# A decoder layer on one core: wide operands for part of the gate/up products, and a new order

## The chip, the cores and the metric

The kernel runs on one core of a Trainium2 chip. A core has engines with instruction streams of their own: TensorE (PE in the profile; its weight loads are PEld), VectorE (DVE), ScalarE (ACT), GpSimd (POOL) and SyncE (SP), which issues most DMAs. The metric is the device time of one execution in microseconds. Lower is better.

## The reference

One layer, float32, on 512 tokens of width 1024: a half-step SwiGLU FFN, two attention groups of eight heads each (native sparse attention and stick-breaking attention) with one output projection, cross-attention to a memory of 256 tokens, and a second half-step FFN.

```python
def swiglu(h, wg, wu, wd):
    return (jax.nn.silu(h @ wg) * (h @ wu)) @ wd
...
x = x + 0.5 * swiglu(rms_norm(x, ffn1_norm[l]), ffn1_wg[l], ffn1_wu[l], ffn1_wd[l])
h = rms_norm(x, mix_norm[l])
...
x = x + jnp.concatenate([o_nsa, o_sb], axis=-1) @ w_out[l]
x = x + memory_cross_attention(rms_norm(x, mem_x_norm[l]), ...)
x = x + 0.5 * swiglu(rms_norm(x, ffn2_norm[l]), ffn2_wg[l], ffn2_wu[l], ffn2_wd[l])
```

The FFNs' inner width is 2816, which is 22 blocks of 128 columns.

## The kernel before

**Precision.** Activations and weights are kept transposed, with 128 channels on the partitions. A float32 operand is split into a high part, rounded to TensorE's fp32r type by a copy on ACT, and a low part, the rest, by a subtraction on DVE (`wsplit`, L580, for weights). One product is three matmuls (`mm3`, L629): high x high, high x low (both with the weight's high part as stationary operand) and low x high.

**Direct blocks.** `ffn_up` (L825) computes a block of gate and up with eight 128-row steps each, three matmuls of 512 columns per step.

**Winograd blocks.** Most blocks of gate and up go through `wino_up` (L904), a seven-product scheme of the Strassen-Winograd kind: the 1024 inner rows are cut in two halves, the 512 tokens in two halves, and gate and up are the two output rows. `right` (L842) makes the seven activation operands b11, b21, b22, t1 to t4 from the normed input, for four steps d each, in two halves ("a" needs the first 256 tokens, "b" all). The weight sums s1 to s4 are DVE additions. `prod` (L886) runs four steps of `mm3` with 256 columns each. The products go to three PSUM banks: X takes b11, then t2, then t3 on top of each other; Y takes b21 and t4 in its two halves; Z takes t1 and then b22. Between them the kernel reads X and Z into SBUF (`take`, L944, and the additions after it), by ACT copies or DVE additions of 256 columns. For 16 blocks of the second FFN the gate's two products (b11, b21) are made early by `wino_gate` (L891).

**Down products.** `ffn_down` (L964) multiplies a group of finished blocks (GROUPS, L68) with one of eight weight units and adds to x.

**Order.** Nothing runs in the order written. A `Planner` (L122 to L521) collects all operations, simulates engines with costs in ns, and emits one fixed instruction order per engine; this is why nearly all instructions carry line 521. Priorities come from the order in which parts are listed: FIRST (L28) for the direct blocks and the operands a0 to b3 of the first FFN, FEED (L71) for the blocks, down products ("0.4" is group 0, unit 4) and stored units ("cw:7") of each FFN, MIDDLE (L83) for attention and the early gates of the second FFN. In FEED a block with a number below that of the direct blocks is skipped. A stored unit (`store_parts`, L592) is loaded and split during the first FFN, and its parts are written to DRAM; later `unit` (L603) loads the parts without splitting.

**PSUM.** Eight banks: two of kind "mm" (X, odd down products), five of "at" (Y, Z, even down products and the attention), one of "sm".

Of the kernel before, what the change touches and what calls it, by code (L numbers as in the profile page):

```python
# [9 lines left out]
F32R = mybir.dt.float32r  # L10
# [17 lines left out]
FIRST = "up up a0 a1 up up b1 up a3 a2 b2 b0 b3"  # L28
# [39 lines left out]
GROUPS = {"1": (6, 8, 8), "2": (8, 8, 6)}  # L68


FEED = {"1": """6 5 ws:1 0.4 cw:7 0.3 18 9 7 wn:1 13 0.5 11 20 10 cw:6 12 0.1 mo:0 0.7 0.2 cw:2 14 0.6 0.0 cw:4 8 17  # L71
15 cw:1 19 1.4 mo:1 1.7 mq:0 16 ws:0 21 1.5 1.1 1.2 ws:2 2.2 1.0 cw:0 mn 2.0 1.3 wn:0 2.7 1.6 2.5 mq:1 2.4 2.1 ws:3 mk
cw:3 2.3 wn:2 2.6 mv wn:3 cw:5""",
        "2": """3 10 4 5 1 2 7 0 6 20 19 0.2 15 0.5 11 17 8 0.4 0.6 16 9 0.1 14 12 13 0.0 1.6 1.0 0.3 1.1 21 1.2 18 2.2 1.5
0.7 2.0 1.3 1.4 2.6 1.7 2.5 2.3 2.1 2.4 2.7"""}
# [7 lines left out]
MIDDLE = """sb_proj.2 sb_values sb_head.2.0 sb_head.2.1 rope sb_proj.3 cmp_mlp.0 sb_proj.0 sb_head.3.1 sb_head.3.0  # L83
sb_head.0.1 cmp_keys sb_proj.1 sb_head.1.1 nsa_query.1 nsa_query.2 nsa_query.3 sb_head.1.0 nsa_query.0 sb_head.0.0
query_rotate nsa_key.1 nsa_key.0 key_rotate cmp_mlp.1 nsa_values nsa_scores.0.0 nsa_scores.1.0 cmp_values
nsa_scores.1.1 nsa_compressed.1 nsa_compressed.2 nsa_scores.0.1 nsa_out.1.1 nsa_compressed.0 nsa_scores.2.0
nsa_out.0.1 nsa_out.0.0 nsa_scores.3.1 nsa_out.1.0 nsa_scores.2.1 nsa_out.2.1 wout_sb wout_nsa.0 nsa_out.2.0
nsa_compressed.3 nsa_scores.3.0 nsa_out.3.1 mem_query.0.0 nsa_out.3.0 mem_query.0.1 mem_head.0.0.1 mem_head.0.1.1
mem_head.0.0.0 mem_head.0.1.0 mem_out.0 wout_nsa.1 right.0.0 right.0.1 mem_query.1.1 right.0.2 right.0.3 gate.15
mem_head.1.1.1 mem_query.1.0 mem_head.1.0.0 mem_head.1.0.1 mem_head.1.1.0 gate.18 gate.8 gate.1 gate.10 mem_out.1  # L90
gate.16 gate.17 gate.6 gate.19 gate.20 gate.11 gate.21 gate.14 right.1.0 gate.13 right.1.1 gate.9 gate.12 right.1.2
right.1.3"""
# [38 lines left out]
class Planner:  # L131
# [15 lines left out]
    NEAR = 20  # L147
    DMA_NS, DMA_GBPS, STORE = 2700, 300, 1.6
# [189 lines left out]
    def attempt(self, hold):  # L338
# [33 lines left out]
        port = {}  # L372

# [27 lines left out]
        while len(out) < len(ops):  # L401
            for e in engines:
                while busy[e] <= now:
# [39 lines left out]
                    if e == "tensor":  # L443
                        tick = int(now / self.TICK_NS)
                        if columns.get(tick - 1, 0) < self.TICK_COLUMNS:
                            ns *= 2
                        columns[tick] = columns.get(tick, 0) + op.columns
# [76 lines left out]
class Kernel:  # L524
# [317 lines left out]
    def right(self, B, gcol, r, half, d):  # L842
# [17 lines left out]
        for i, e in enumerate((d, d + 4)):  # L860
            nc.vector.scalar_tensor_tensor(h[:, i * H:(i + 1) * H], self.x[e][:, hc], self.gm[:, gcol + e:gcol + e + 1],
                                           r[:, hc], OP.mult, OP.mult)
        if half == 0:
            B["h", d] = h
            q = self.pair()
            parts(h, *q)
            B["b11", d], B["b21", d] = [t[:, :H] for t in q], [t[:, H:] for t in q]
            return
        b11, b21, b12, b22 = B["h", d][:, :H], B["h", d][:, H:], h[:, :H], h[:, H:]
        if ("b22", d ^ 1) not in B:  # L870
            B["b22", "both", d // 2] = self.pair()
        B["b22", d] = [t[:, d % 2 * H:(d % 2 + 1) * H] for t in B["b22", "both", d // 2]]
        parts(b22, *B["b22", d])
# [6 lines left out]
        for src, n0, n1 in ((t12, "t1", "t2"), (t34, "t3", "t4")):  # L880
            q = self.pair()
            parts(src, *q)
            B[n0, d] = q[0][:, :H], q[1][:, :H]
            B[n1, d] = q[0][:, H:], q[1][:, H:]

    def prod(self, ps, w, B, b, first=True):  # L886
        for i in range(4):
# [90 lines left out]
    def ffn(self, k, B, As, early, pre, done):  # L978


        for part in FEED[k].split():
# [11 lines left out]
            elif n >= pre:  # L993
                self.wino_up(k, n, B, As[n], early.get(n))
# [891 lines left out]
```

## Time and profile before

| | |
|---|---|
| median of three runs | 1064.45 us (1062.35 to 1064.98) |
| profiled execution: its span from the first to the last instruction (the page gives no other time of it) | 1060.7 us |
| mean granted TensorE clock | 0.994 |
| PE busy | 1042.9 us, 6708 matmuls |
| weight loads busy | 948.3 us, 6708 |
| DVE busy | 906.6 us, 1904 instructions |
| ACT busy | 660.8 us, 1383 instructions |
| HBM | 136.40 MB read, 23.07 MB written |

The first FFN fills the span to about 340 us, the middle goes to about 700, early gates and the second FFN fill the rest. Matmuls are pipelined, so the recorded length of one is longer than its distance from the next; distances between starts say what one costs. Records of DVE and ACT instructions in a row overlap a little as well. A row of a timeline is: start in us, length in us, engine, line, operation, output<-inputs by the program's names (p is PSUM, t an SBUF tile, w and raw weight tiles, half a half-width tile), partitions x elements, and the count of instructions merged into it.

### The profile page before, as it was taken

The page shows a single profiled execution, that of the slowest core. Times are in us where ns is not written, and L with a number is a line of the kernel's source. Part 1 is how long each engine was busy: PE and PEld are TensorE (multiplying, and loading weights), DVE is VectorE, ACT ScalarE, POOL GpSimd, SP SyncE. Part 2 cuts the span into 40 slices and gives each one's busy share as a digit, 9 for nine tenths or more (in the row PEclk, how much of TensorE's full clock was granted, in tenths as well). Part 3 has the DMA queues.
Part 4 walks back from the last instruction along what each step waited for, and adds up shares of the span by engine and source line. Part 5 has one row for each costly group of instructions (what it writes and reads, how often), then busy time and mean ns, then how long its engine had stood idle before and what let it go on. Part 6 is the DMA issues. An engine that isn't in the chain of part 4 may idle for free.

```text
span 1060.7 us, 19227 instructions
## 1 busy us (share of the span) xinstructions
PE 1042.9 (98%) x6708; PEld 948.3 (89%) x6708; DVE 906.6 (85%) x1904; ACT 660.8 (62%) x1383; POOL 47.3 (4%) x88
## 2 busy tenths in 40 slices
PE   9999999999999999899989999999999999999998
PEld 7899999998988888788878889899999999998887
DVE  8998988898956977988899988899999999885632
ACT  8565665565744858889867868787566545452420
POOL 0000000000000000000003442110000000000000
PEclk9999999999999999999989999999999999999999
DMA  8336537548767833510357263356333444442321
GB/s 278 104 97 203 174 114 249 179 150 281 247 229 244 290 98 118 192 59 10 120 159 230 61 218 121 111 175 210 110 123 120 130 149 134 132 143 86 119 93 50
DMA packets 92881, 162.06 MB, mean 153 GB/s; under 512 B 11248, under 2 KB 17008, under 8 KB 92784
## 3 DMA queue, kind: packets, MB, share of 16 engines
q1 hardware_dynamic: 92352, 160.54, 47.2%
q8 instruction: 53, 0.87, 0.3%
q14 instruction: 44, 0.36, 0.1%
q10 hardware_dynamic: 432, 0.29, 0.1%
HBM read 136.40 MB, written 23.07 MB: 150 GB/s over the span
## 4 chain that ended last, share of the span: by engine, by line
PE 85%; DVE 8%; DMA 3%; ACT 2%; issue 1%; SPq 0%; ACTq 0%; DVEq 0%
PE p L521 85%; DVE t L521 4%; DVE s L521 2%; ACT t L521 2%; DMA raw<-in_ws_dram 2%; DMA d<-w 1%; DVE w L521 1%; DVE raw L521 1%; ACT w L521 0%; DVE gates L521 0%; SPq L521 0%; ACTq L521 0%; ACT L516 0%; DVEq L521 0%
## 5 line engine op out<-in xcount | busy, mean ns | idle before, releaser
L521 PE MATMUL p<-t,w 128*128 128x256 f32 (+1 forms) x5502 | 885.0, 319 | 4.5 <-ACT t L521 1.7
L521 PEld LDWEIGHTS p<-t,w 128*128 128x128 f32 x5502 | 780.5, 190 | 75.9 <-DVE t L521 4.3
L521 ACT ACTIVATE w<-raw 128x512 fp32r<-128x512 f32 (+1 forms) x450 | 267.7, 613 | 204.2 <-PE p L521 123.1
L521 DVE TENSOR_TENSOR w<-raw,w 128x512 fp32r<-128x512 f32 (+1 forms) x450 | 295.5, 671 | 78.6 <-issue 27.8
L521 ACT ACTIVATE t<-t 128x512 f32<-128x512 f32 (+7 forms) x424 | 214.2, 533 | 68.0 <-DVE t L521 63.8
L521 DVE TENSOR_TENSOR t<-t,t 128x512 fp32r<-128x512 f32 (+8 forms) x332 | 186.8, 578 | 10.6 <-ACT t L521 8.7
L521 ACT ACTIVATE t<-p 128x256 f32<-128x256 f32 (+5 forms) x156 | 75.2, 504 | 37.4 <-PE p L521 35.7
L521 PE MATMUL p<-t,t 128*128 128x256 f32 (+4 forms) x450 | 93.7, 333 | 0.4 <-ACT t L521 0.3
L521 DVE SCALAR_TENSOR_TENSOR t<-p,t 128x512 f32<-128x512 f32 (+3 forms) x107 | 66.3, 629 | 29.0 <-PE p L521 24.5
L521 DVE TENSOR_TENSOR t<-p,t 128x256 f32<-128x256 f32 (+4 forms) x159 | 82.2, 536 | 7.9 <-PE p L521 3.7
L521 PEld LDWEIGHTS p<-t,t 128*128 128x128 f32 x450 | 71.4, 190 | 10.0 <-ACT t L521 1.6
L521 DVE TENSOR_TENSOR raw<-raw,raw 128x512 f32<-128x512 f32 (+1 forms) x94 | 59.1, 635 | 0.9
L521 DVE TENSOR_TENSOR t<-p,half 128x256 f32<-128x256 f32 x117 | 45.8, 416 | 4.9 <-PE p L521 2.3
L521 POOL TENSOR_SCALAR t<-t,s 128x256 f32<-128x256 f32 (+3 forms) x80 | 44.6, 580 | 110.8 <-DVE s L521 48.9
L521 PE MATMUL p<-w,t 128*128 128x512 f32 (+2 forms) x240 | 40.8, 330 | 0.2 <-DVE s L521 0.2
L521 PEld LDWEIGHTS p<-w,t 128*128 128x128 f32 x240 | 36.3, 189 | 4.1 <-issue 0.4
L521 PE MATMUL p<-cr,t 128*128 128x128 f32 (+2 forms) x256 | 37.9, 265 | 0.2 <-ACT t L521 0.2
L521 ACT ACTIVATE w<-w 128x512 fp32r<-128x512 f32 x39 | 24.5, 627 | 20.3 <-DVE w L521 11.8
L521 PEld LDWEIGHTS p<-cr,t 128*128 128x128 f32 x256 | 31.3, 152 | 3.6 <-ACT t L521 0.6
L521 ACT ACTIVATE t<-t,g 128x256 fp32r<-128x256 f32 (+1 forms) x40 | 23.5, 587 | 13.7 <-DVE t L521 11.7
L521 PE MATMUL p<-t,cr 128*128 128x512 f32 (+4 forms) x114 | 30.5, 332 | 0.5 <-DVE t L521 0.5
L521 ACT ACTIVATE half<-p 128x256 f32<-128x256 f32 x46 | 17.3, 377 | 17.6 <-PE p L521 17.3
(82 smaller groups left out, 439.8 us busy)
## 6 DMA issues: line engine op xcount, KB each, us to landing
raw<-in_ws_dram SPq DMA_DIRECT2D x364, 256.0 KB, 3.0
w<-d SPq DMA_DIRECT2D x112, 256.0 KB, 3.2
d<-w SPq DMA_DIRECT2D x80, 256.0 KB, 3.9
raw<-in_wraw_dram SPq DMA_DIRECT2D x16, 256.0 KB, 3.0
raw<-in_ws_dram SPq DMA_DIRECT2D x22, 128.0 KB, 3.0
t<-in_xT_dram SPq DMA_DIRECT2D x8, 256.0 KB, 4.9
out_dram<-t SPq DMA_DIRECT2D x7, 256.0 KB, 2.0
t<-in_memT_dram SPq DMA_DIRECT2D x8, 128.0 KB, 4.4
```

The source lines that it names most:

```text
L521: return getattr(getattr(self.nc, op.eng), method)(*args, **kw)
```

## The change

A new table WIDE names, per FFN and block, which banks become wide: "x" is X, "z" is X and Z, "-" none. The activation operands now lie in one 512-column tile each, high part on the left, low part on the right. For a wide bank a step of `prod` issues one matmul of 512 columns (the weight's high part against both parts) and one of 256 (the weight's low part against the high part, added to the right half). The left half of the bank then holds the sums and the right half the corrections, and `whole` adds the two while it evacuates. `right` splits its results in halves of 256 columns, each into a tile of its own. FIRST has six "up" instead of five, so 16 blocks of the first FFN instead of 17 go through Winograd; 15 of them and 8 of the second FFN are wide somewhere, 23 in all. GROUPS of the second FFN is cut 8, 7, 7 instead of 8, 8, 6. FEED, MIDDLE and the list of stored units (qn:3 is new among them) have a new order; FEED's block 0 to 5 entries of the first FFN are skipped. The planner's cost of a 256-column matmul after a wide one is 6 ns less. The assertions check only the order of the lists.

```diff
--- before.py
+++ after.py
@@ -25,7 +25,7 @@
 NCMP = 31
 
 
-FIRST = "up up a0 a1 up up b1 up a3 a2 b2 b0 b3"
+FIRST = "up a0 up up up a1 b1 a3 up a2 up b2 b3 b0"
 NBIG = 74
 NWARM = 7
 KEEP = 4
@@ -65,14 +65,17 @@
            "compressed": "vector", "softmax": "gpsimd", "abs": "vector scalar",
            "double": "vector scalar gpsimd"}
 
-GROUPS = {"1": (6, 8, 8), "2": (8, 8, 6)}
-
-
-FEED = {"1": """6 5 ws:1 0.4 cw:7 0.3 18 9 7 wn:1 13 0.5 11 20 10 cw:6 12 0.1 mo:0 0.7 0.2 cw:2 14 0.6 0.0 cw:4 8 17
-15 cw:1 19 1.4 mo:1 1.7 mq:0 16 ws:0 21 1.5 1.1 1.2 ws:2 2.2 1.0 cw:0 mn 2.0 1.3 wn:0 2.7 1.6 2.5 mq:1 2.4 2.1 ws:3 mk
-cw:3 2.3 wn:2 2.6 mv wn:3 cw:5""",
-        "2": """3 10 4 5 1 2 7 0 6 20 19 0.2 15 0.5 11 17 8 0.4 0.6 16 9 0.1 14 12 13 0.0 1.6 1.0 0.3 1.1 21 1.2 18 2.2 1.5
-0.7 2.0 1.3 1.4 2.6 1.7 2.5 2.3 2.1 2.4 2.7"""}
+GROUPS = {"1": (6, 8, 8), "2": (8, 7, 7)}
+
+
+WIDE = {"1": "zzx--xxxxxxxxx-xxxxxxz", "2": "-x--x-x----xz---zzx---"}
+
+
+FEED = {"1": """0 wn:1 3 ws:0 10 14 mo:1 8 18 0.4 cw:7 0.3 7 13 6 ws:1 0.5 20 9 cw:6 12 4 11 0.7 2 mo:0 cw:2 0.6 0.2 0.1 0.0 cw:4 19
+17 cw:1 15 1.4 wn:0 1.5 16 1.2 1 mq:0 21 5 1.7 2.2 1.1 1.0 mn cw:0 1.3 2.0 ws:2 mk qn:3 2.7 2.5 2.4 mq:1 2.1 1.6 2.3
+cw:3 wn:2 ws:3 2.6 mv wn:3 cw:5""",
+        "2": """3 4 10 7 0 5 2 1 6 21 0.2 14 11 0.5 12 0.6 16 15 0.7 9 8 0.1 0.3 20 17 13 1.2 19 1.6 0.0 1.5 18 1.4 2.2 0.4 1.0 1.3
+2.4 2.0 1.1 2.3 2.5 1.7 2.1 2.7 2.6"""}
 
 UNITS = [("1g", NF), ("1u", NF), ("1d", ND * len(GROUPS["1"])), ("vs", 4), ("sq", 4), ("sk", 4), ("ks", 1), ("kw", 1), ("vg", 4),
          ("kc", 1), ("vc", 1), ("qn", 4), ("ws", 4), ("mk", 2), ("mv", 2), ("wn", 4), ("mq", 2), ("mo", 2),
@@ -80,16 +83,15 @@
 UNIT_AT = {n: sum(k for _, k in UNITS[:i]) for i, (n, _) in enumerate(UNITS)}
 
 
-MIDDLE = """sb_proj.2 sb_values sb_head.2.0 sb_head.2.1 rope sb_proj.3 cmp_mlp.0 sb_proj.0 sb_head.3.1 sb_head.3.0
-sb_head.0.1 cmp_keys sb_proj.1 sb_head.1.1 nsa_query.1 nsa_query.2 nsa_query.3 sb_head.1.0 nsa_query.0 sb_head.0.0
-query_rotate nsa_key.1 nsa_key.0 key_rotate cmp_mlp.1 nsa_values nsa_scores.0.0 nsa_scores.1.0 cmp_values
-nsa_scores.1.1 nsa_compressed.1 nsa_compressed.2 nsa_scores.0.1 nsa_out.1.1 nsa_compressed.0 nsa_scores.2.0
-nsa_out.0.1 nsa_out.0.0 nsa_scores.3.1 nsa_out.1.0 nsa_scores.2.1 nsa_out.2.1 wout_sb wout_nsa.0 nsa_out.2.0
-nsa_compressed.3 nsa_scores.3.0 nsa_out.3.1 mem_query.0.0 nsa_out.3.0 mem_query.0.1 mem_head.0.0.1 mem_head.0.1.1
-mem_head.0.0.0 mem_head.0.1.0 mem_out.0 wout_nsa.1 right.0.0 right.0.1 mem_query.1.1 right.0.2 right.0.3 gate.15
-mem_head.1.1.1 mem_query.1.0 mem_head.1.0.0 mem_head.1.0.1 mem_head.1.1.0 gate.18 gate.8 gate.1 gate.10 mem_out.1
-gate.16 gate.17 gate.6 gate.19 gate.20 gate.11 gate.21 gate.14 right.1.0 gate.13 right.1.1 gate.9 gate.12 right.1.2
-right.1.3"""
+MIDDLE = """sb_proj.2 sb_values sb_head.2.0 sb_head.2.1 sb_proj.3 rope cmp_mlp.0 sb_proj.0 sb_head.3.1 sb_head.3.0 sb_head.0.1
+cmp_keys sb_proj.1 sb_head.1.1 nsa_query.2 nsa_query.1 nsa_query.3 sb_head.1.0 nsa_query.0 sb_head.0.0 query_rotate
+nsa_key.1 nsa_key.0 cmp_mlp.1 key_rotate nsa_values nsa_scores.0.0 nsa_scores.1.1 nsa_scores.1.0 cmp_values
+nsa_compressed.1 nsa_out.1.1 nsa_scores.0.1 nsa_compressed.2 nsa_compressed.0 nsa_scores.2.0 nsa_out.0.0 nsa_out.0.1
+nsa_out.1.0 nsa_scores.3.1 nsa_scores.2.1 wout_sb nsa_out.2.1 wout_nsa.0 nsa_out.2.0 nsa_compressed.3 nsa_scores.3.0
+nsa_out.3.1 nsa_out.3.0 mem_query.0.1 mem_query.0.0 mem_head.0.0.1 mem_head.0.1.0 mem_head.0.1.1 mem_head.0.0.0
+mem_out.0 wout_nsa.1 right.0.0 right.0.1 right.0.3 mem_query.1.1 right.0.2 gate.15 mem_query.1.0 mem_head.1.0.0
+mem_head.1.0.1 mem_head.1.1.0 gate.18 mem_head.1.1.1 gate.1 mem_out.1 gate.16 gate.6 gate.8 gate.19 gate.11 gate.17
+gate.14 right.1.0 gate.13 gate.20 right.1.1 gate.9 gate.21 right.1.3 gate.12 gate.0 right.1.2"""
 
 
 HOLD = """sb_head.3.0>sb_head.3.1 sb_head.1.1>sb_head.3.0"""
@@ -145,6 +147,7 @@
 
     ROWS_NS = {"vector": 115, "scalar": 118, "gpsimd": 112}
     NEAR = 20
+    HIDDEN_NS = 6
     DMA_NS, DMA_GBPS, STORE = 2700, 300, 1.6
 
     TICK_NS, TICK_COLUMNS = 10240 / 3, 3060
@@ -370,6 +373,7 @@
         columns = {}
         rows = {e: (0, 0) for e in engines}
         port = {}
+        wide = False
 
         def fits(op):
             new = [n for n in op.tiles if n not in opened]
@@ -441,6 +445,9 @@
                             ns += self.ROWS_NS[e]
                         rows[e] = op.rows
                     if e == "tensor":
+                        if wide and op.columns == T // 2:
+                            ns -= self.HIDDEN_NS
+                        wide = op.columns >= T
                         tick = int(now / self.TICK_NS)
                         if columns.get(tick - 1, 0) < self.TICK_COLUMNS:
                             ns *= 2
@@ -860,43 +867,69 @@
         for i, e in enumerate((d, d + 4)):
             nc.vector.scalar_tensor_tensor(h[:, i * H:(i + 1) * H], self.x[e][:, hc], self.gm[:, gcol + e:gcol + e + 1],
                                            r[:, hc], OP.mult, OP.mult)
+        def both(src, n0, n1):
+            for n, t in ((n0, src[:, :H]), (n1, src[:, H:])):
+                q = self.t2(F32R)
+                parts(t, q[:, :H], q[:, H:])
+                B[n, d] = q
+
         if half == 0:
             B["h", d] = h
-            q = self.pair()
-            parts(h, *q)
-            B["b11", d], B["b21", d] = [t[:, :H] for t in q], [t[:, H:] for t in q]
+            both(h, "b11", "b21")
             return
         b11, b21, b12, b22 = B["h", d][:, :H], B["h", d][:, H:], h[:, :H], h[:, H:]
-        if ("b22", d ^ 1) not in B:
-            B["b22", "both", d // 2] = self.pair()
-        B["b22", d] = [t[:, d % 2 * H:(d % 2 + 1) * H] for t in B["b22", "both", d // 2]]
-        parts(b22, *B["b22", d])
+        B["b22", d] = q = self.t2(F32R)
+        parts(b22, q[:, :H], q[:, H:])
         t12, t34 = self.t2(), self.t2()
 
         minus(t12[:, :H], b11, b12)
         negative(t12[:, H:], t12[:, :H], b22)
         minus(t34[:, :H], b22, b12)
         negative(t34[:, H:], t12[:, H:], b21)
-        for src, n0, n1 in ((t12, "t1", "t2"), (t34, "t3", "t4")):
-            q = self.pair()
-            parts(src, *q)
-            B[n0, d] = q[0][:, :H], q[1][:, :H]
-            B[n1, d] = q[0][:, H:], q[1][:, H:]
+        both(t12, "t1", "t2")
+        both(t34, "t3", "t4")
 
     def prod(self, ps, w, B, b, first=True):
+
+        nc = self.nc
+        H = T // 2
         for i in range(4):
             k = slice(i * P, (i + 1) * P)
-            self.mm3(ps, (w[0][:, k], w[1][:, k]), B[b, i], first and i == 0, i == 3)
+            x = B[b, i]
+            if ps.shape[1] == H:
+                self.mm3(ps, (w[0][:, k], w[1][:, k]), (x[:, :H], x[:, H:]), first and i == 0, i == 3)
+            else:
+                nc.tensor.matmul(ps, w[0][:, k], x, start=first and i == 0, stop=False, skip_group_check=True)
+                nc.tensor.matmul(ps[:, H:], w[1][:, k], x[:, :H], start=False, stop=i == 3, skip_group_check=True)
+
+    def whole(self, out, ps, more=None):
+
+        nc = self.nc
+        H = T // 2
+        if ps.shape[1] == T:
+            if more is None:
+                nc.scalar.activation(out, ps[:, H:], AF.Copy)
+            else:
+                nc.vector.tensor_tensor(out, ps[:, H:], more, OP.add)
+            nc.vector.tensor_tensor(out, ps[:, :H], out, OP.add)
+        elif more is None:
+            nc.scalar.activation(out, ps, AF.Copy)
+        else:
+            nc.vector.tensor_tensor(out, ps, more, OP.add)
+
+    def bank(self, k, f, which, tag):
+        ps = self.ps(tag)
+        return ps if WIDE[k][f] in {"x": "xz", "z": "z"}[which] else ps[:, :T // 2]
 
     def wino_gate(self, k, f, B):
 
         nc = self.nc
         H = T // 2
         raw = self.load(k + "g", f)
-        X, Y = self.ps("mm")[:, :H], self.ps("at")[:, :H]
+        X, Y = self.bank(k, f, "x", "mm"), self.ps("at")[:, :H]
         t = self.t2()
         self.prod(X, self.wsplit(raw[0]), B, "b11")
-        nc.scalar.activation(t[:, H:], X, AF.Copy)
+        self.whole(t[:, H:], X)
         self.prod(Y, self.wsplit(raw[1]), B, "b21")
         nc.vector.tensor_tensor(t[:, :H], Y, t[:, H:], OP.add)
         return t
@@ -927,12 +960,12 @@
             return t
 
         a21, a22 = self.load(k + "u", f, (1,) if dma else (0, 1))
-        X, Y, Z = self.ps("mm")[:, :H], self.ps("at"), self.ps("at")[:, :H]
+        X, Y, Z = self.bank(k, f, "x", "mm"), self.ps("at"), self.bank(k, f, "z", "at")
         u2, u3 = [self.wtile("half", F32, NHALF, (P, H)) for _ in range(2)]
         if not early:
             gt = self.t2()
             self.prod(X, self.wsplit(a11), B, "b11")
-            nc.scalar.activation(gt[:, H:], X, AF.Copy)
+            self.whole(gt[:, H:], X)
             self.prod(Y[:, :H], self.wsplit(a12), B, "b21")
             nc.vector.tensor_tensor(gt[:, :H], Y[:, :H], gt[:, H:], OP.add)
         s1 = dma_sum(in_u[:, :T], in_u[:, T:]) if dma else add(a21, a22)
@@ -942,21 +975,18 @@
         self.prod(X, self.wsplit(s2), B, "t2", first=early)
 
         def take(u):
-            if early:
-                nc.vector.tensor_tensor(u, X, gt[:, H:], OP.add)
-            else:
-                nc.scalar.activation(u, X, AF.Copy)
+            self.whole(u, X, gt[:, H:] if early else None)
 
         take(u2)
         self.prod(Z, self.wsplit(s1), B, "t1")
         self.prod(X, self.wsplit(s3), B, "t3", first=False)
         take(u3)
         ut = self.t2()
-        nc.vector.tensor_tensor(ut[:, H:], Z, u3, OP.add)
+        self.whole(ut[:, H:], Z, u3)
         nc.vector.tensor_tensor(ut[:, :H], Y[:, H:], u3, OP.add)
         s4 = add(a12, s2, a12)
         self.prod(Z, self.wsplit(s4), B, "b22", first=False)
-        nc.vector.tensor_tensor(gt[:, H:], Z, u2, OP.add)
+        self.whole(gt[:, H:], Z, u2)
         nc.scalar.activation(gt, gt, AF.Silu)
         nc.vector.tensor_tensor(ut, ut, gt, OP.mult)
         self.split(ut, a[0], a[1])
@@ -978,6 +1008,7 @@
     def ffn(self, k, B, As, early, pre, done):
 
 
+        ready = {}
         for part in FEED[k].split():
             if part in self.memory:
                 self.memory[part]()
@@ -988,10 +1019,14 @@
                 continue
             n, *j = [int(i) for i in part.split(".")]
             if j:
+                assert all(f < pre or f in ready for f in range(sum(GROUPS[k][:n]), sum(GROUPS[k][:n + 1])))
+                ready[j[0], "d"] = ready.get((j[0], "d"), 0) + 1
+                assert n < len(GROUPS[k]) - 1 or ready[j[0], "d"] == len(GROUPS[k])
                 self.ffn_down(k, n, j[0], As[sum(GROUPS[k][:n]):sum(GROUPS[k][:n + 1])],
                               lambda h: done(j[0], h) if n == len(GROUPS[k]) - 1 else None)
             elif n >= pre:
                 self.wino_up(k, n, B, As[n], early.get(n))
+                ready[n] = True
 
     def pair(self):
         return self.t2(F32R), self.t2(F32R)
@@ -1705,7 +1740,17 @@
             d["tv", qt] = self.nsa_compressed(qt, [q[b] for b in range(4)], d["f"], d["kc"], d["gates"])
             d["no", qt] = self.t2().rearrange("p (b q) -> p b q", b=4)
 
+        def mn():
+            self.mem_norm()
+
+        def mk():
+            self.mem_keys()
+
+        def mv():
+            self.mem_values()
+
         def nsa_scores(qt, g):
+            assert "first" in kk
             d["s", qt, g] = self.nsa_scores(qt, g, [q[b] for b in range(4)], d["f"], kk, d["gates"])
 
         def nsa_out(qt, g):
```

## The prediction

> **What bounds the kernel now.** I read the page's head first, then its chain that ended last, then a table by stage.
>
> ```profile
> span 1060.7 us, 19227 instructions
> PE 1042.9 (98%) x6708; PEld 948.3 (89%) x6708; DVE 906.6 (85%) x1904; ACT 660.8 (62%) x1383; POOL 47.3 (4%) x88
> ...
> PE 85%; DVE 8%; DMA 3%; ACT 2%; issue 1%; SPq 0%; ACTq 0%; DVEq 0%
> ```
>
> PE (TensorE) is busy for 98% of the span and owns 85% of the chain. A busy PE is not a PE at its peak, so the table by stage follows; its columns are the stretch in us, its length, then the busy time and instructions of PE, weight loads, DVE, ACT and POOL, the granted clock, the DMA share and GB/s.
>
> ```profile
> 0.00:75.00 75.00, 73.05 (x365) 61.31 (x366) 70.08 (x142) 50.31 (x93) 0.21 (x4) 1.00 0.47 151
> 75.00:340.00 265.00, 264.60 (x1787) 245.75 (x1787) 221.42 (x394) 152.79 (x297) 0.00 (x0) 1.00 0.63 207
> ...
> 430.00:450.00 20.00, 16.14 (x85) 14.04 (x84) 19.41 (x54) 16.48 (x37) 0.00 (x0) 0.91 0.62 201
> 450.00:535.00 85.00, 85.00 (x452) 73.18 (x450) 74.52 (x159) 74.31 (x157) 0.80 (x1) 1.00 0.24 74
> 535.00:560.00 25.00, 21.05 (x143) 20.17 (x143) 24.50 (x61) 15.16 (x33) 1.23 (x2) 0.80 0.51 161
> 560.00:700.00 140.00, 137.13 (x924) 122.76 (x923) 127.90 (x386) 109.20 (x301) 39.49 (x72) 1.00 0.48 151
> 700.00:875.00 175.00, 174.79 (x1405) 171.95 (x1404) 172.91 (x358) 111.84 (x231) 5.13 (x8) 1.00 0.45 141
> 875.00:925.00 50.00, 50.00 (x363) 47.39 (x362) 46.04 (x85) 23.24 (x40) 0.00 (x0) 1.00 0.41 127
> 925.00:1061.00 136.00, 132.08 (x739) 115.61 (x737) 75.74 (x133) 40.97 (x70) 0.00 (x0) 1.00 0.32 101
> ```
>
> Three things are to be seen. In the first FFN (0 to 340) PE never rests after its start, while DVE (VectorE) has 265 - 221.4 = 43.6 us of idle time from 75 on. From 700 to 875, where the second FFN's early gates and its first blocks lie, PE (174.8 of 175) and DVE (172.9 of 175) are both full: this stage has two bounds. The middle loses PE time at 430 to 450 and 535 to 560, and there the granted clock is 0.91 and 0.80.
>
> What does a matmul cost where PE never rests? The timeline shows three pieces: 116 matmuls of 512 columns in a row, 59 of 256 columns in a row, and a place in the middle where both kinds alternate. Columns: start, length, engine, operation, count.
>
> ```profile
> 23.71 26.45 PE L521 MATMUL p<-t,w 128*128 128x512 f32 x116
> ...
> 139.03 7.24 PE L521 MATMUL p<-t,w 128*128 128x256 f32 x59
> ...
> 412.87 0.39 PE L521 MATMUL p<-t,w 128*128 128x512 f32 x1
> 413.11 0.27 PE L521 MATMUL p<-t,cr 128*128 128x256 f32 x1
> 413.22 0.40 PE L521 MATMUL p<-t,w 128*128 128x512 f32 x1
> 413.45 0.34 PE L521 MATMUL p<-t,cr 128*128 128x384 f32 x1
> ...
> 422.95 0.28 PE L521 MATMUL p<-t,cr 128*128 128x256 f32 x1
> 423.07 0.40 PE L521 MATMUL p<-t,w 128*128 128x512 f32 x1
> 423.31 0.34 PE L521 MATMUL p<-t,cr 128*128 128x384 f32 x1
> ```
>
> The last of each row lasts its own 0.39 or 0.28 us, so the spacing is (26.45 - 0.39)/115 = 226.6 ns for 512 columns and (7.24 - 0.28)/58 = 120.0 ns for 256. The difference, 106.6 ns, is what 256 columns take to stream; 120.0 - 106.6 = 13.4 ns is a price per matmul that doesn't depend on its width. Every matmul has its own weight load (x6708 of both).
>
> **The change, part by part.**
>
> *1. Wide operands.* In a wide product each of four steps issues one 512-column matmul and one of 256 columns, where it issued three of 256: as many columns, one matmul and one weight load less. Wide X means three products of a block, wide X and Z five. Counting the letters of WIDE for the blocks that go through Winograd: first FFN, blocks 6 to 21, 14 x and 1 z; second FFN, 5 x and 3 z. Steps: (19 x 3 + 4 x 5) x 4 = 308. Three matmuls took 360.0 ns. If the fixed price is paid per matmul, the pair costs 226.6 + 120.0 = 346.6 and the step saves 13.4 ns. The alternating rows bound it: from 413.11 to 413.45 a 256 and a 512 took 0.34, from 412.87 to 413.22 0.35, from 422.95 to 423.31 0.36 us. So a step saves from 20 ns down to nothing. I take 13.4, which is also what the middle one of the three rows gives within its rounding: 308 x 13.4 ns = **-4.1 us**; ends -6.2 and 0.
>
> On that fixed price the Trainium skill ("TensorE: Matmul & The Clock Gate", "Back-to-back issue gap") speaks against the change: a warm matmul starts N/2.4 + 2.5 ns after the one before. By it a step would save only 2.5 ns, 308 of them 0.8 us. The trace's 13.4 ns differs, and the measurement decides.
>
> *2. One block more goes the direct way.* FIRST holds six "up" instead of five, and FEED skips blocks below that number, so 16 blocks instead of 17 go through Winograd. A direct block has 2 x 8 x 3 = 48 matmuls of 512 columns, 10.88 us; a Winograd block 7 x 4 x 3 = 84 of 256, 10.08 us: **+0.8 us** of PE.
>
> *3. More work for DVE.* A wide bank holds the sums on its left and the corrections on its right half, so each evacuation gets one more DVE addition of 256 columns: 3 per x, 5 per z, 77 in all, 47 in the first FFN and 30 in the second. ACT's copies stay as many. The prices, from the timeline of DVE where it runs without a pause:
>
> ```profile
> 799.77 0.68 DVE L521 TENSOR_TENSOR w<-raw,w 128x512 fp32r<-128x512 f32 x1
> 800.37 0.41 DVE L521 TENSOR_TENSOR t<-p,half 128x256 f32<-128x256 f32 x1
> 800.70 0.68 DVE L521 TENSOR_TENSOR w<-raw,raw 128x512 f32<-128x512 f32 x1
> 801.30 0.41 DVE L521 TENSOR_TENSOR half<-p,t 128x256 f32<-128x256 f32 x1
> ```
>
> Start to start, 512 columns take 0.60 us and 256 take 0.33. A Winograd block now costs DVE 7 low parts, 4 weight sums, a product and a low part of the result at 0.60, and 4 evacuations at 0.33: 13 x 0.60 + 4 x 0.33 = 9.1 us against 10.08 us of PE. A wide x block needs 10.1 us against 10.08 - 0.16 = 9.9: alone it would be bound by DVE, and lives on the down products, which need little DVE. The direct block needs 4 low parts, 2 evacuations, a product and a low part, 8 x 0.60 = 4.8 us, so part 2 frees 9.1 - 4.8 = 4.3 us. The operands of "right" are split in halves of their own: per d three 512-column pairs of copy and subtraction become six of 256, 12 more instructions per FFN on each of DVE and ACT; DVE pays 2 x 0.33 - 0.60 = 0.06 us for each, 0.7 us.
>
> In the first FFN that makes 47 x 0.33 + 0.7 - 4.3 = 11.9 us, and 1.2 us of part 4. What hides it is DVE's 43.6 idle us from 75 on; without this cover it would cost up to 13.1 us. In the second FFN it makes 30 x 0.33 + 0.7 = 10.6 us. Of the early gates 18, 1, 16, 6, 11, 17 and 0 are wide (one addition each, 2.3 us), and blocks that FEED names late carry the z. The cover is 50 - 46.0 = 4 us of idle DVE from 875 to 925 and 136 - 75.7 = 60 us after it; before 875 there are only 2. I take **0**, because PE can be given down products (three matmuls of 0.227 us for each of 22 x 8 weight pieces) while DVE catches up; the end for the range is the part of the 10.6 us that lies before 925.
>
> *4. One more stored unit.* qn:3 is split in the first FFN and written to DRAM, and nsa_query.3 loads its parts instead of splitting.
>
> ```profile
> w<-d SPq DMA_DIRECT2D x112, 256.0 KB, 3.2
> d<-w SPq DMA_DIRECT2D x80, 256.0 KB, 3.9
> ```
>
> It adds four stores and four loads, 2 MB, on SP's queue; the two raw loads come earlier. Stores are behind nothing that PE waits for, and DMA is at 0.63 in the fullest stretch. It takes two low parts (1.2 us of DVE) and two copies out of 450 to 535, ahead of the longest wait of PE. That wait, and the chain up to it:
>
> ```profile
> PE p L521 <- issue: 6.5, 3, 3.7
> ...
> 529.37 1.68 ACT t L521 x3
> ...
> 531.07 1.68 ACT t L521 x3
> ...
> 533.33 1.90 DVE t L521 x3
> ...
> 536.62 1.20 DVE t L521 x2
> ```
>
> From 529 to 543 the chain that ended last runs through ACT and DVE, not PE, so work taken from their queues before it can shorten the 3.7 us. Ends 0 and -1.2; I take **-0.8**, nearer to the full price because both engines are taken off.
>
> *5. The order.* MIDDLE swaps neighbours (rope after sb_proj.3, cmp_mlp.1 ahead of key_rotate, gate.0 in place of gate.10). Such swaps move the stalls of the middle, and I know no sign: **0**. The ends come from the two stretches with a low clock: 25 us at 0.80 is 5.0 us lost, 20 us at 0.91 is 1.8. One more of the larger kind costs 5 us, one less gives 5 back. GROUPS of the second FFN as 8, 7, 7 changes the sizes of the down products and not their sum: 22 x 8 x 3 matmuls and 24 evacuations as before; 0.
>
> Sum: -4.1 + 0.8 + 0 - 0.8 + 0 = -4.1 us. The page gives the profiled execution's span, 1060.7 us, and no other time of its own; the runs' median, 1064.45, lies 3.8 us above. The sum makes the span 1056.6 and the runs 1064.45 - 4.1 = **1060.4 us**.
>
> **The rivals.**
>
> *A: the pair saves nothing.* The 0.36 us row is the rule once the order alternates all the time. For it: two of three alternating rows are above 0.346. Against it: they mix in matmuls of other weights and banks. Then -0 + 0.8 - 0.8 = 0: 1064.4 us.
> The rule of the Trainium skill in part 1 ("TensorE: Matmul & The Clock Gate", "Back-to-back issue gap") leads to nearly the same, 0.8 us below this; by the rows of part 1 the price per matmul is 13.4 ns, which speaks against it.
>
> *B: the order helps the middle more.* One low-clock stretch like that at 535 to 560 goes away: 1060.4 - 5.0 = 1055.4. For it: DVE and ACT get room just there. Against it: cmp_mlp's small work, which leaves PE without matmuls, is all still there.
>
> *C: the order brings one more.* 1060.4 + 5.0 = 1065.4.
>
> *D: DVE becomes the bound from 700 to 925.* For it: 172.9 of 175 us. Up to 925 I count 7 gate additions, some 13 of blocks 4, 1, 6, 11 and 12, and the 0.7 us of "right": 20 x 0.33 + 0.7 = 7.3 us. An evacuation that comes late holds its PSUM bank, the next product into that bank is queued in PE's fixed order, and everything behind it waits. If nothing absorbs it, 1060.4 + 7.3 = 1067.7: slower. It decides from 4.1 us of unabsorbed delay on. Against it: from 875 DVE has gaps again while PE has none, so today DVE is ahead of PE at the end of that stretch.
>
> **How the numbers follow.** This kernel's three runs lie within 0.25%, so 0.3%, 3.2 us, is about what can be told from no change. My forecast gets 0.45, A 0.14, B 0.16, C 0.11, D 0.14. The forecast's own range is 1058.5 to 1062.5. It lies 0.9 us beyond the line of 1061.25, so 0.32 of its 0.45 is faster by over 0.3% and 0.13 within. A: 0.02 and 0.12. B is all faster. C: 0.07 within, 0.04 slower. D ends beyond 1067.6 only if nothing is absorbed: 0.03 within, 0.11 slower. Together 0.50 faster, 0.35 within, 0.15 slower. The range reaches from just below B to just short of D: 1054.5 to 1067.
>
> **What would show it.** Part 1: some 344 matmuls fewer (308 from the steps, 36 from part 2), and in a wide block a spacing of 0.347 us for a 512 and a 256. Part 2: six blocks of 512-column matmuls at the start. Part 3: 77 new DVE additions of 256 columns from PSUM, DVE's busy time up by some 20 us, and PE still at 174 or more in a stretch of 175 ahead of 875. Part 4: "d<-w" x84 and "w<-d" x116, and a wait on "issue" below 3.7 us. I am wrong if the alternating spacing is 0.36, if PE shows waits for DVE between 700 and 925, or if the low-clock stretches grow.

## The result and the profile after

The changed kernel takes 1057.0 us (median, 1055.2 to 1057.8) against 1064.7 us before: a ratio of 0.993 with a 95% interval from 0.9911 to 0.9949, so 5.4 to 9.5 us shorter, 7.5 in the middle. The forecast was 4.1 us shorter. In a later set of runs (e9) it took 1055.3, a ratio of 0.9924 (0.9911 to 0.9937). The two medians go with the granted clock: of the nine executions, four at a mean clock of 0.995 have a median of 1057.4 us and five at 0.997 one of 1055.2. The kernel before never rose above 0.995 in the later sets; at 0.995 its medians were 1063.3 to 1063.8 (and no longer at 0.993). So at an equal clock the gain is about 6 us, and up to 2 us more go with the clock.

The head, the chain and two DMA rows of the page after:

```profile
span 1054.8 us, 18662 instructions
PE 1040.2 (99%) x6367; PEld 931.9 (88%) x6367; DVE 922.0 (87%) x1989; ACT 662.5 (63%) x1404; POOL 48.1 (5%) x92
...
PE 91%; DVE 5%; DMA 1%; issue 1%; ACT 1%; SPq 0%; DVEq 0%; ACTq 0%
...
w<-d SPq DMA_DIRECT2D x116, 256.0 KB, 3.1
d<-w SPq DMA_DIRECT2D x84, 256.0 KB, 3.8
```

There are 6708 - 6367 = 341 matmuls fewer (344 were expected; a few records of a trace can be missing), DVE has 85 instructions and 15.4 us more, and the chain runs through PE for 91% of the span instead of 85%. The table by stage, with the same columns as before:

```profile
75.00:340.00 265.00, 264.33 (x1637) 237.53 (x1636) 236.37 (x451) 159.67 (x313) 0.39 (x1) 1.00 0.61 193
...
430.00:450.00 20.00, 17.52 (x93) 15.49 (x92) 18.68 (x53) 16.80 (x38) 0.00 (x0) 0.91 0.48 161
450.00:535.00 85.00, 85.00 (x461) 73.70 (x459) 75.57 (x160) 77.41 (x164) 0.84 (x1) 1.00 0.31 97
535.00:560.00 25.00, 21.32 (x154) 20.54 (x153) 24.53 (x69) 14.87 (x29) 2.23 (x3) 0.86 0.57 167
560.00:700.00 140.00, 138.65 (x947) 126.26 (x946) 129.67 (x392) 112.69 (x313) 40.69 (x75) 1.00 0.49 157
700.00:875.00 175.00, 174.35 (x1325) 167.25 (x1325) 174.16 (x368) 109.56 (x230) 3.73 (x8) 1.00 0.44 134
875.00:925.00 50.00, 50.00 (x322) 45.28 (x321) 49.09 (x95) 23.14 (x40) 0.00 (x0) 1.00 0.44 137
```

From 75 to 340 DVE's idle time shrank from 43.6 to 28.6 us; from 700 to 925 it is down from 6.0 to 225 - 223.25 = 1.75 us, and PE still runs. The middle lost less: the granted clock from 535 to 560 is 0.86 instead of 0.80. What PE waited for, before and then after (total us, times, longest):

```profile
PE p L521 <- issue: 6.5, 3, 3.7
PE p L521 <- ACT t L521: 3.6, 5, 1.5
PE p L521 <- DVE t L521: 3.2, 6, 1.1
PE p L521 <- ACT w L521: 0.8, 1, 0.8
PE p L521 <- DVE s L521: 0.5, 2, 0.3
```

```profile
PE p L528 <- issue: 5.4, 2, 2.9
PE p L528 <- DVE t L528: 2.6, 5, 1.1
PE p L528 <- ACT t L528: 1.9, 3, 0.9
PE p L528 <- ACT w L528: 0.7, 1, 0.7
PE p L528 <- ACT half L528: 0.5, 1, 0.5
```

The waits sum to 14.6 and 11.1 us. I also took from both traces the distance of each matmul's start to the next, less its columns at 106.6 ns per 256 and less the 13.4 ns. The spans differ by 5.9 us. Of it 3.3 us come from fewer matmuls (by the prediction's own prices), about 1.3 us are lost again by spacings that are a little longer than these prices, and about 4 us come from what is over 60 ns, near to the 3.5 us by which the sum of the waits fell. So the profile has two gains, about 2 us in the matmuls and 3.5 to 4 us in waits and in matmuls at a low clock; where the cut of 60 ns is set moves some tenths between the two. Of the second gain, 3.7 us arose between 340 and 560 and 2.3 between 560 and 700; the first 25 us and the FFN stages lost 2.1 of that. The spans differ by less than the medians: in the runs after, a time lies 1.8 us above its span, so the profiled execution of before was probably the 1062.35, the fastest of its four.

### The profile page after: what moved, and what is told of

Same layout as the page of the kernel before. It is cut to its first block, busy times and chain, and to the rows that moved or that the text cites. A ratio compares the mean times of both kernels' runs of the same rounds, so it can differ in the third digit from the quotient of the medians.

```text
span 1054.8 us, 18662 instructions
## 1 busy us (share of the span) xinstructions
PE 1040.2 (99%) x6367; PEld 931.9 (88%) x6367; DVE 922.0 (87%) x1989; ACT 662.5 (63%) x1404; POOL 48.1 (5%) x92
## 4 chain that ended last, share of the span: by engine, by line
PE 91%; DVE 5%; DMA 1%; issue 1%; ACT 1%; SPq 0%; DVEq 0%; ACTq 0%
PE p L528 91%; DVE t L528 3%; DVE w L528 2%; DMA raw<-in_ws_dram 1%; DMA d<-w 0%; ACT t L528 0%; DVE raw L528 0%; DMA g<-in_gains_dram 0%; ACT w L528 0%; DVE s L528 0%; SPq L528 0%; ACT half L528 0%; DVE half L528 0%; DVEq L528 0%; DVE one L528 0%
## 5 line engine op out<-in xcount | busy, mean ns | idle before, releaser
L528 PEld LDWEIGHTS p<-t,w 128*128 128x128 f32 x5161 | 763.9, 190 | 91.8 <-DVE t L528 3.2
L528 ACT ACTIVATE w<-raw 128x512 fp32r<-128x512 f32 (+1 forms) x448 | 264.4, 614 | 195.8 <-PE p L528 102.2
L528 ACT ACTIVATE t<-t 128x512 f32<-128x512 f32 (+9 forms) x445 | 216.2, 514 | 73.4 <-DVE t L528 69.0
L528 DVE TENSOR_TENSOR t<-t,t 128x512 f32<-128x512 f32 (+9 forms) x356 | 189.5, 550 | 9.0 <-ACT t L528 6.8
L528 DVE TENSOR_TENSOR t<-p,t 128x256 f32<-128x256 f32 (+5 forms) x189 | 94.5, 517 | 6.8 <-ACT t L528 3.5
L528 POOL TENSOR_SCALAR t<-t,s 128x256 f32<-128x256 f32 (+3 forms) x80 | 43.6, 564 | 109.7 <-DVE s L528 54.7
L528 POOL CAST t<-t 64x512 fp32r<-64x512 f32 (+2 forms) x8 | 4.3, 539 | 551.6 <-DVE t L528 336.6
```

Source lines behind the costliest of these rows:

```text
L528: return getattr(getattr(self.nc, op.eng), method)(*args, **kw)
```

## Experiments

The planner works out a new order whenever a list, a cost or an operation changes, so most edits also change the order everywhere. Two experiments (e5, e6) therefore alter an instruction only when it is issued: the order of every engine stays the same. In the three sets of runs (e1 to e4, e5 to e8, e9 to e12) the kernel before had medians of 1062.9, 1063.0 and 1064.0 us; distances to the changed kernel below are to its 1055.3 of e9, four of whose five executions had the clock of 0.997.

**The wide operand against the lists.**

e1 has all new lists and no wide operand:

```diff
-WIDE = {"1": "zzx--xxxxxxxxx-xxxxxxz", "2": "-x--x-x----xz---zzx---"}
+WIDE = {"1": "-" * 22, "2": "-" * 22}
```

> The changed kernel with every letter of WIDE set to '-': all lists new, no wide operand. Theory 1 (most of the gain is the new order; a wide step saves only about 7 ns, since the changed kernel's own trace has a median of 351 ns for a 512 and a 256 column matmul in a row): 308 x 7 ns = 2.2 us longer than the changed kernel, about 1059, and the middle as short as there. Rival (the wide operand carries the gain): back to 1063 or more.

Measured: 1062.9 us, ratio 0.9993 (0.9981 to 1.0004). No gain is left, where theory 1 had 1059; taken alone this speaks for the rival.

e2 has the wide operand and the lists of before, of which FIRST is shown; GROUPS, FEED and MIDDLE go back likewise:

```diff
-FIRST = "up a0 up up up a1 b1 a3 up a2 up b2 b3 b0"
+FIRST = "up up a0 a1 up up b1 up a3 a2 b2 b0 b3"
```

> The changed kernel's code and WIDE with FIRST, GROUPS, FEED and MIDDLE of before (five direct blocks; 80 x 4 = 320 wide steps, since block 5 goes through Winograd and is an x): the wide operand without the new order. Theory 1: 320 x 7 ns = 2.2 us less than before at best, and DVE additions that nobody made room for: 1062 to 1066. Rival (the wide operand carries the gain): 1057 to 1059.

Measured: 1075.6 us, ratio 1.0102 (1.0076 to 1.0128): 11 us slower than before, outside both expectations. Its waits of PE:

```profile
PE p L529 <- DVE t L529: 7.6, 11, 2.1
PE p L529 <- issue: 6.3, 2, 3.9
```

Waits for DVE's t tiles were 3.2 us before. PE was busy for 309.4 of the 315 us from 25 to 340, where it had been 314.6: the first FFN now has gaps.

So neither part gains anything alone, though each of the two runs also has an order of its own. The next run holds the order fixed and undoes only the wide matmul; the 512-column matmul of a wide step carries the mark `halves`, and the code that issues it reads:

```diff
+        if kw.pop("halves", False):
+            out, w, x = args
+            for c in (slice(0, T // 2), slice(T // 2, T)):
+                self.nc.tensor.matmul(out[:, c], w, x[:, c], **kw)
+            return
```

> The changed kernel with the same fixed order on every engine; only where a 512-column matmul of a wide step is issued, two of 256 columns stand in its place. So three matmuls and three weight loads per step again, with all else as it is. Theory 2 (in the kernel a wide step saves 7 ns, since there three matmuls take 360 and the pair 353): 308 x 7 ns = 2.2 us longer than the changed kernel. Rival (a price of 13.4 ns per matmul): 4.1 us longer. Second rival (the pair saves nothing, as it nearly did behind the end of the kernel, 353.3 against 353.8): no difference.

Both halves carry the mark that starts an accumulation, where the wide matmul has it once, and the kernel no longer computes the layer; number, size and order of the matmuls are as the diff says, and it stands here for its time alone. Measured: 1058.2 us, ratio 0.9947 (0.9935 to 0.996).

> The changed kernel once more, to have its ratio to the kernel before beside those of the other runs, above all of the one with halves for wide matmuls (ratio 0.9947). Theory 2 (7 ns per wide step, 2.2 us): ratio 0.9926, about 1055.3 where before is at 1063. Rival (13.4 ns, 4.1 us): 0.9908. Second rival (nothing saved): 0.9947.

Measured for the changed kernel itself: 1055.3 us, ratio 0.9924 (0.9911 to 0.9937). The difference of the ratios is 0.0023, 2.4 us of 1063; the two intervals together leave room from about 0.5 to 4.3 us. At the same mean clock of 0.997, four executions of the changed kernel and three of e5 are 2.6 us apart. The intervals would also let 4.1 us pass, but only just; the spacings decide. In the changed kernel's trace three 256-column matmuls in a row took 360 ns (median of some 2400 places), a 512 and a 256 behind another 256 a median of 350 and, gaps left out, a mean of 353 (281 places). 308 x 7 ns = 2.2 us. The rows of the stage from 25 to 340, of e5 and of the changed kernel's second profile:

```profile
25.00:340.00 315.00, 314.03 (x2041) 288.01 (x2040) 286.68 (x561) 191.06 (x377) 0.39 (x1) 1.00 0.57 188
```

```profile
25.00:340.00 315.00, 313.25 (x1853) 277.98 (x1852) 285.80 (x560) 190.93 (x377) 0.39 (x1) 1.00 0.57 188
```

188 matmuls and weight loads less in the same 315 us: weight loads fall from 288 to 278 us, PE stays full. The load that is saved was mostly hidden.

What a step costs with everything else quiet was measured behind the end of the changed kernel: 80 steps of three matmuls, 80 of a pair, and both again, on constant weights.

```diff
+            for i in range(n):
+                first, end = i % 4 == 0, i % 4 == 3
+                if wide:
+                    nc.tensor.matmul(out, w[0], q, start=first, stop=False, skip_group_check=True)
+                    nc.tensor.matmul(out[:, H:], w[1], q[:, :H], start=False, stop=end, skip_group_check=True)
+                else:
+                    self.mm3(out, w, (q[:, :H], q[:, H:]), first, end)
```

> The changed kernel with rows of steps behind its end, on constant weights and the last tile of x: 80 steps of three 256-column matmuls, 80 steps of a 512 and a 256, and both once more, with ACT, DVE and DMA quiet. Theory 1 (alternation itself costs more than a price per matmul): three take 360 ns, the pair 350 to 352. Rival (the fixed price is paid once per matmul, and other engines disturb it in the kernel): the pair takes 346.6.

The table by stage, for a stretch of threes and one of pairs:

```profile
1055.00:1075.00 20.00, 20.00 (x172) 20.00 (x171) 0.00 (x0) 0.00 (x0) 0.00 (x0) 1.00 0.01 2
1081.00:1105.00 24.00, 24.00 (x137) 20.93 (x136) 0.00 (x0) 0.00 (x0) 0.00 (x0) 1.00 0.00 1
```

171 weight loads in 20 us and 136 in 24 us: 351 ns for three, 353 ns for a pair, to within a load at the edges. By the single starts both take 353.3 ns, the first step of each row left out. So the pair takes what it takes in the kernel, and saves nothing here, because here three 256-column matmuls take 353 and not 360. The rival's 346.6 is out. Within the pairs the spacings repeat, 236, 119, 231, 117, 233 and 124 ns: the 512s, at 231 to 236, take longer than the 226.6 of the long row of 512s in the kernel before. The Trainium skill ("TensorE: Matmul & The Clock Gate", "Back-to-back issue gap") gives N/2.4 + 2.5 ns for an isolated matmul, and says that in a stream with a weight load for each matmul both set the spacing. The prediction left that condition out. The estimate of 2.5 ns per step that it worked out from the formula is more than this row shows and less than the kernel's 7.

**The order.**

e3 puts the old MIDDLE into the changed kernel, e7 the new MIDDLE into the kernel before. Two lines of the list, as e3 changes them:

```diff
-nsa_key.1 nsa_key.0 cmp_mlp.1 key_rotate nsa_values nsa_scores.0.0 nsa_scores.1.1 nsa_scores.1.0 cmp_values
+query_rotate nsa_key.1 nsa_key.0 key_rotate cmp_mlp.1 nsa_values nsa_scores.0.0 nsa_scores.1.0 cmp_values
...
```

> The changed kernel with MIDDLE of before. Theory 1 (the gain lies in the stalls of the middle and is made by its new list): 4 to 7 us longer than the changed kernel, 1061 to 1064, with the PE waits of the stretch from 430 to 560 as before. Rival (the middle is better because qn:3 is stored, or because of what comes before it): 1057 to 1058.

Measured: 1059.8 us, ratio 0.9968 (0.9957 to 0.9979): 4.5 us longer than the changed kernel's 1055.3, the distance that theory 1 had, though not its 1061 to 1064. Its reason holds only in part. PE's waits sum to 15.4 us, which is 4.3 and 3.7 more than in the two profiles of the changed kernel (11.1 and 11.7). Of that 0.9 and 1.5 lie between 340 and 560, where the waits are 7.4 us (8.8 in the kernel before); the rest lies in other stages, from 25 to 340 too, ahead of the work that MIDDLE lists. So an edit of this list changes the order everywhere, and the 4.5 us are not what the list does to the middle alone.

> The kernel before with MIDDLE of the changed kernel and nothing else. Theory 2 (the new list itself has fewer stalls in the middle): 3 to 5 us less than before, 1058 to 1060. Rival (a list fits only the kernel that it was made for): no gain or a loss against before.

Measured: 1066.4 us, ratio 1.0028 (1.0018 to 1.0038): 3 us slower than before. The rival holds: the new list is not a better list. That it fits the new kernel is one reading; the other is that a new order comes out some us longer or shorter, whatever the list (e8 and e10 below). The four longest waits of PE in e7 (its profile is of the fastest of ten executions) and e3:

```profile
PE p L520 <- issue: 6.6, 2, 4.1
PE p L520 <- ACT t L520: 4.9, 4, 2.0
PE p L520 <- DVE t L520: 4.4, 8, 1.1
PE p L520 <- ACT w L520: 0.6, 1, 0.6
```

```profile
PE p L529 <- issue: 6.3, 2, 3.8
PE p L529 <- DVE t L529: 5.1, 9, 1.2
PE p L529 <- ACT t L529: 2.6, 3, 1.5
PE p L529 <- ACT w L529: 0.8, 2, 0.7
```

16.5 and 14.8 us, where the two kernels with a list of their own have 14.6 and 11.1 in all.

e8 leaves all work and all lists as they are and alters one cost in the planner:

```diff
-    HIDDEN_NS = 6
+    HIDDEN_NS = 0
```

> The changed kernel with the planner's HIDDEN_NS at 0 instead of 6: the same work and lists, and an order that the planner works out from a slightly other cost. Theory 2 (the gain sits in one order that fits these lists and costs, and any other costs several us of stalls): 2 to 6 us longer than the changed kernel, with the same nominal matmul time. Rival (the lists carry the gain, whatever the order in detail): within 1 us of it.

Measured: 1063.8 us, ratio 1.0009 (0.9999 to 1.0019): 8.5 us longer than the changed kernel, beyond theory 2's 6, with the same 6367 matmuls recorded, and the whole gain is gone. Its longest waits of PE, from a profile of the slowest of its ten executions:

```profile
PE p L528 <- issue: 6.4, 2, 3.9
PE p L528 <- DVE t L528: 5.4, 10, 1.2
PE p L528 <- DMA t<-t: 1.5, 1, 1.5
```

So two orders of the same work are 8 us apart here, more than the wide operand's 2.2 us.

e10 keeps the lists of before and no wide operand; only the operands' layout is new:

```diff
-            B["b11", d], B["b21", d] = [t[:, :H] for t in q], [t[:, H:] for t in q]
+            both(h, "b11", "b21")
```

> The lists of before, no wide operand, and of the change only the layout of the activation operands: one tile each, made in halves of 256 columns, 24 more instructions on DVE and on ACT. Theory 3 (each part is worth little by itself): 1 us longer to 3 us shorter than before. Rival (finer halves let products start earlier and carry the gain): 5 us or more shorter than before.

Measured: 1060.5 us, ratio 0.9971 (0.9959 to 0.9982), 3.1 us shorter and just past the end of theory 3's span. PE's waits shrank from 8.8 to 4.5 us between 340 and 560, where no such operand is made, and from 25 to 340, where the first set is made, they went from 0.4 to 0.2. The clock in the middle rose too: the rows of e10 for the stretches that had 0.91 and 0.80 before are

```profile
430.00:450.00 20.00, 17.51 (x100) 15.28 (x99) 19.43 (x54) 17.30 (x39) 0.00 (x0) 1.00 0.50 169
...
535.00:560.00 25.00, 23.61 (x148) 21.34 (x148) 24.31 (x70) 14.05 (x32) 2.45 (x4) 0.87 0.44 131
```

Its six executions go with their mean clock, from 1062.4 us at 0.995 to 1059.6 at 0.998; at 0.995 the kernel before had 1063.8. That speaks for another order and its clock by chance and not for the layout, but they were not separated.

**DVE as the second bound.**

e6 repeats a piece of work for DVE ahead of each of the 77 additions, in the fixed order:

```diff
+        if kw.pop("twice", False):
+            for c in (slice(0, P), slice(P, 2 * P)):
+                self.nc.vector.tensor_tensor(self.spare, args[1][:, c], args[2][:, c], OP.add)
```

> The changed kernel with the same fixed order; ahead of each of the 77 new DVE additions two more of 128 columns on the same operands into a spare tile, some 0.4 us each time, 31 us of DVE in all. Theory 2 (DVE is a second bound in the first FFN and from 700 to 925, and only the order gives it room): 5 to 15 us longer, with PE waiting for DVE there. Rival (idle DVE time hides it, as the prediction took for the 77 themselves): under 2 us.

Measured: 1102.2 us, ratio 1.0363 (1.0349 to 1.0378): 47 us longer than the changed kernel, three times the upper end of theory 2. Its busy times and longest waits of PE:

```profile
PE 1057.6 (96%) x6367; PEld 934.5 (85%) x6367; DVE 965.5 (88%) x2143; ACT 662.4 (60%) x1404; POOL 49.0 (4%) x92
```

```profile
PE p L532 <- DVE t L532: 18.0, 40, 1.1
PE p L532 <- DVE half L532: 8.5, 18, 1.1
```

DVE became busier by 965.5 - 922.0 = 43.5 us (the small additions cost more than I had put down), and the kernel 47 us longer. Idle DVE time hid none of it, though DVE was still idle for over 130 us. The waits grew where the additions are: from 25 to 340 PE waited 17.4 us (0.5 in the changed kernel's first profile) and from 700 to 925 8.1 (0.7). Per addition that is 0.56 us more work and 0.61 us more time, as if each evacuation stood directly ahead of a matmul whose place is fixed.

e11 goes back to five direct blocks:

```diff
-FIRST = "up a0 up up up a1 b1 a3 up a2 up b2 b3 b0"
+FIRST = "up a0 up up up a1 b1 a3 up a2 b2 b3 b0"
-FEED = {"1": """0 wn:1 3 ws:0 10 14 mo:1 8 18 0.4 cw:7 0.3 7 13 6 ws:1 0.5 20 9 cw:6 12 4 11 0.7 2 mo:0 cw:2 0.6 0.2 0.1 0.0 cw:4 19
-17 cw:1 15 1.4 wn:0 1.5 16 1.2 1 mq:0 21 5 1.7 2.2 1.1 1.0 mn cw:0 1.3 2.0 ws:2 mk qn:3 2.7 2.5 2.4 mq:1 2.1 1.6 2.3
+FEED = {"1": """5 0 wn:1 3 ws:0 10 14 mo:1 8 18 0.4 cw:7 0.3 7 13 6 ws:1 0.5 20 9 cw:6 12 4 11 0.7 2 mo:0 cw:2 0.6 0.2 0.1 0.0 cw:4 19
+17 cw:1 15 1.4 wn:0 1.5 16 1.2 1 mq:0 21 1.7 2.2 1.1 1.0 mn cw:0 1.3 2.0 ws:2 mk qn:3 2.7 2.5 2.4 mq:1 2.1 1.6 2.3
```

> The changed kernel with five direct blocks instead of six; block 5 stands first in FEED, goes through Winograd and is an x. PE has 0.8 us less to do and 0.1 us less for 12 wide steps, DVE 5.3 us more. Theory 3 (DVE is the second bound of the first FFN): 5 to 12 us longer than the changed kernel, with PE stalls between 25 and 340. Rival (PE alone is the bound there): 0.9 us shorter.

Measured: 1070.5 us, ratio 1.0066 (1.0052 to 1.008): 15 us longer, beyond theory 3's 12. PE lost 315 - 306.3 = 8.7 us from 25 to 340, against 1.75 in the second profile of the changed kernel:

```profile
25.00:340.00 315.00, 306.34 (x1838) 272.21 (x1837) 282.74 (x555) 184.69 (x367) 0.00 (x0) 0.99 0.56 184
```

This speaks for the direct block, which costs PE more, as what makes room for the wide ones; e2, which has five direct blocks too, lost in the same stretch. Only part of the 15 us lies there, and the order is another as well.

e12 takes qn:3 out of the stored units:

```diff
-17 cw:1 15 1.4 wn:0 1.5 16 1.2 1 mq:0 21 5 1.7 2.2 1.1 1.0 mn cw:0 1.3 2.0 ws:2 mk qn:3 2.7 2.5 2.4 mq:1 2.1 1.6 2.3
+17 cw:1 15 1.4 wn:0 1.5 16 1.2 1 mq:0 21 5 1.7 2.2 1.1 1.0 mn cw:0 1.3 2.0 ws:2 mk 2.7 2.5 2.4 mq:1 2.1 1.6 2.3
```

> The changed kernel without qn:3 among the stored units, which nsa_query.3 then loads and splits itself. The prediction's step: 0 to 1.2 us longer than the changed kernel, with PE's wait for cmp_mlp at about 3.7 instead of 2.9 us. Rival (an order worked out anew costs more than the step itself): 2 to 7 us longer, with the added stalls in other places than that wait.

Measured: 1061.7 us, ratio 0.9985 (0.9973 to 0.9997): 6.4 us longer than the changed kernel. The longest wait on "issue" is 4.1 us, 1.0 more than in the second profile after:

```profile
PE p L528 <- issue: 7.1, 3, 4.1
PE p L528 <- DVE t L528: 4.0, 6, 1.7
PE p L528 <- DVE w L528: 1.5, 2, 1.1
```

The rival's span holds: from 340 to 560 PE waited 9.8 us against 6.0 in the second profile of the changed kernel, 1.5 of it for DVE's w tiles (weights being split), for which the changed kernel waits nowhere. The wait on "issue" grew by about what was predicted for the step. How much of the 6.4 us the step makes and how much the new order was not separated.

## Why the prediction was right, and where it was not

The direction and the range held; the gain was 7.5 us where the forecast said 4.1, and the sum got there by terms of other sizes. In part this was luck: 1057.0 lies outside the forecast's own 1058.5 to 1062.5 and nearer to rival B, and with the wide operand at its measured 2.2 us the same sum gives 1062.3, less than 0.3% below the kernel before. What is left over, more than half of the gain, came by the term that stood at 0.

*1. Wide operands, -4.1:* right in kind, too large. It was the 13.4 ns that failed: the price per matmul is not independent of its neighbours. A pair takes 353 ns (350 in the median) and not 346.6, the gain is 2.2 us (2.4 by e5 and e9), inside the bounds 0 and 6.2. The three alternating rows of before, 0.34, 0.35 and 0.36 us, had the right value as their mean; I chose the model over it.

*2. One block more the direct way, +0.8:* its matmuls are in the count. What it is worth to DVE was only a side remark in part 3; without it e11 took 15 us more, part of which may be its order.

*3. DVE's additions at 0:* the 77 additions came as counted (DVE's busy time rose by 15.4 us, not by some 20), and PE's waits for DVE hardly changed (3.7 us before, 2.6 and 3.7 in the two profiles after). One of the seven early gates was misread: WIDE has block 12 wide and not block 0, the count is right. The reason I gave for the 0 is wrong. I took 43.6 us of idle DVE time as cover; in e6, in a fixed order, idle time covered nothing of the work that was added. With the old lists (e2) the kernel with the additions was 11 us slower than before, with waits for DVE. That they are hidden because the new lists put other matmuls in front of PE is likely, but no run shows it. Rival D named this mechanism but put it at 700 to 925; with the old lists most of what PE lost anew lay in the first FFN, 315 - 309.4 = 5.6 us from 25 to 340 (0.4 before), against 1.9 (0.2 before) from 700 to 925.

*4. qn:3 at -0.8:* the wait went from 3.7 to 2.9 us, as expected, and e12 has 4.1 without the step. What the step gave can't be told from what the order did to the same wait.

*5. The order at 0:* this is the term that was missed. Waits fell by 3.5 us in the profile, mostly between 340 and 700. Rival B's direction was right, its mechanism, one low-clock stretch less, only in part: from 535 to 560 the clock rose from 0.80 to 0.86, 1.5 us over 25, and in the executions at 0.997 about 2 us more went with the clock. The rest is shorter waits. That this part of the gain sits in one order for these costs, not in the lists, is what e7 and e8 speak for; which of the shorter waits the order made, and whether the clock follows the waits or the waits the clock, stays open.

## What to carry to other kernels

Where two engines are nearly full and the order is fixed, price an instruction that is added ahead of an evacuation on the second engine at its full length, not at zero because of idle time elsewhere: 43.5 us of DVE cost 47 us. When the order was worked out anew for the additions, as in the change itself, they could be hidden. Separate an edit from its reordering: change the instruction as it is issued and leave the order alone; undone through the planner the wide operand seemed worth 7.6 us, undone in place 2.4. And where a planner turns a 6 ns change of one cost into 8.5 us, ask what re-planning is worth before crediting any part of a change.

## What the runs showed of the hardware

Three 256-column matmuls, each with its weight load, take 360 ns in the running kernel and 353 ns with the other engines quiet and constant weights; the pair of 512 and 256 takes 353 in both. Which of the two differences, the quiet engines or the weights, makes the 7 ns was not tried. The low-clock stretches of the middle (0.91 and 0.80 before, 0.91 and 0.86 after) lie at the two places of the middle where PE waits for cmp_mlp and runs many small matmuls. In the traces the clock is at one half for 3.4 and 10.2 us before, for 3.4 and 6.8 us after. Their lengths changed from kernel to kernel, in e5 the first one is missing with the order unchanged, and what sets them stays open. They are not bound to the middle: e11 and e2 each have another in the first FFN (a clock of 0.57 and 0.67 from 68 to 72 us).
